# Row sums of a 67 MB array: loads of 14 rows per partition instead of 8, three buffers instead of five, and a re-cut end

## Chip, cores, metric

One core of a Trainium2 chip. The three groups of experiments below ran on three different chips (4, 11 and 0), each together with runs of the kernel before; so kernels of different groups are compared by their ratio to that kernel, or by their profiles. The metric is the device time of one execution in microseconds. Some executions of a kernel can fall into a slower state of the chip; every execution named here was in the fast state, except that the state of before_again, a single run, is unknown. The granted clock was 1.0 in all. The profile counts a shorter time, the span (162.9 us for an execution of 164.67 us before), so spans are compared with spans and times with times.

## The reference

```python
x: float32 [32, 512, 1024]          # 67.1 MB
out = np.sum(x, axis=-1) / 1024.0   # float32 [32, 512]
```

The 16,384 rows are laid out as 128 partitions of 128 consecutive rows. Each partition reads its own 512 KB of memory in order and writes 128 sums.

## The kernel before

The array is brought in by 21 loads: fifteen of 8 rows per partition, then 4, 2 and 1 rows, then the last row in three pieces. VectorE (DVE) sums 5 of each 8 rows with one reduction. ScalarE (ACT) sums the other 3 by a copy with an accumulator; the copies go to a scratch buffer in PSUM. SyncE (SP) issues all loads.

```python
bulk = [8] * 15
tail = [4, 2, 1]
pool = ctx.enter_context(tc.tile_pool(name="bulk", bufs=5))
psum = ctx.enter_context(tc.tile_pool(name="junk", bufs=1, space=bass.MemoryType.PSUM))
junk = psum.tile([P, D], F32, name="junk")
# ... cut ...
def act_sum(dst, src):
    n = src.shape[-1]
    nc.scalar.activation(junk[:, :n], src, COPY, accum_out=dst)

def sums(t, j, rows, for_act):
    d = rows - for_act
    if d:
        nc.vector.reduce_sum(out=res[:, j : j + d], in_=t[:, :d, :], axis=AX)
    for r in range(d, rows):
        act_sum(res[:, j + r : j + r + 1], t[:, r, :])

for rows in bulk:
    t = pool.tile([P, 8, D], F32, name="t")
    nc.sync.dma_start(out=t[:, :rows, :], in_=xr[:, j : j + rows, :])
    sums(t, j, rows, rows * 3 // 8)
    j += rows
# ... cut: the loads of 4, 2 and 1 rows, likewise ...
h, q = D // 2, D // 4
last = one.tile([P, D], F32, name="last")
for a, b in ((0, h), (h, h + q), (h + q, D)):
    nc.sync.dma_start(out=last[:, a:b], in_=xr[:, j, a:b])
nc.vector.reduce_sum(out=part[:, 0:1], in_=last[:, 0:h], axis=AX)
act_sum(part[:, 1:2], last[:, h : h + q])
nc.vector.tensor_scalar_mul(out=res[:, :j], in0=res[:, :j], scalar1=scale)
nc.vector.reduce_sum(out=part[:, 2:3], in_=last[:, h + q : D], axis=AX)
nc.vector.reduce_sum(out=part[:, 3:4], in_=part[:, 0:3], axis=AX)
nc.vector.tensor_scalar_mul(out=res[:, j : j + 1], in0=part[:, 3:4], scalar1=scale)
nc.sync.dma_start(out=out_v, in_=res)
```

Of the kernel before, what the change touches and what calls it, by code (L numbers as in the profile page):

```python
# [1 line left out]

# [4 lines left out]

F32 = mybir.dt.float32
ADD = mybir.AluOpType.add
MULT = mybir.AluOpType.mult  # L10
COPY = mybir.ActivationFunctionType.Copy
AX = mybir.AxisListType.X


@with_exitstack
def kernel(
    ctx: ExitStack,
    tc: tile.TileContext,
    x: bass.AP,
    divisor: float,  # L20
    out: bass.AP,
):
    nc = tc.nc
    xf = x.flatten_outer_dims()
    N, D = xf.shape
    P = nc.NUM_PARTITIONS
    scale = 1.0 / float(divisor)
    J = N // P
    assert J * P == N


    xr = x.tensor.reshape((P, J, D)).ap()
    out_v = out.tensor.reshape((P, J)).ap()

    bulk = [8] * 15
    tail = [4, 2, 1]
    assert sum(bulk) + sum(tail) + 1 == J
    pool = ctx.enter_context(tc.tile_pool(name="bulk", bufs=5))
    one = ctx.enter_context(tc.tile_pool(name="one", bufs=1))
    psum = ctx.enter_context(tc.tile_pool(name="junk", bufs=1, space=bass.MemoryType.PSUM))  # L40

    res = one.tile([P, J], F32, name="res")
    part = one.tile([P, 4], F32, name="part")
    junk = psum.tile([P, D], F32, name="junk")

    def act_sum(dst, src):
        n = src.shape[-1]
        nc.scalar.activation(junk[:, :n], src, COPY, accum_out=dst)  # L48

    def sums(t, j, rows, for_act):  # L50
        d = rows - for_act
        if d:
            nc.vector.reduce_sum(out=res[:, j : j + d], in_=t[:, :d, :], axis=AX)  # L53
        for r in range(d, rows):
            act_sum(res[:, j + r : j + r + 1], t[:, r, :])

    j = 0
    for rows in bulk:
        t = pool.tile([P, 8, D], F32, name="t")
        nc.sync.dma_start(out=t[:, :rows, :], in_=xr[:, j : j + rows, :])  # L60
        sums(t, j, rows, rows * 3 // 8)
        j += rows
    for k, rows in enumerate(tail):
        t = one.tile([P, rows, D], F32, name=f"tail{k}")
        nc.sync.dma_start(out=t, in_=xr[:, j : j + rows, :])
        sums(t, j, rows, (rows + 1) // 2)
        j += rows


    h, q = D // 2, D // 4  # L70
    last = one.tile([P, D], F32, name="last")
    for a, b in ((0, h), (h, h + q), (h + q, D)):
        nc.sync.dma_start(out=last[:, a:b], in_=xr[:, j, a:b])
    nc.vector.reduce_sum(out=part[:, 0:1], in_=last[:, 0:h], axis=AX)  # L74
    act_sum(part[:, 1:2], last[:, h : h + q])
    nc.vector.tensor_scalar_mul(out=res[:, :j], in0=res[:, :j], scalar1=scale)  # L76
    nc.vector.reduce_sum(out=part[:, 2:3], in_=last[:, h + q : D], axis=AX)  # L77
    nc.vector.reduce_sum(out=part[:, 3:4], in_=part[:, 0:3], axis=AX)  # L78
    nc.vector.tensor_scalar_mul(out=res[:, j : j + 1], in0=part[:, 3:4], scalar1=scale)  # L79
    nc.sync.dma_start(out=out_v, in_=res)  # L80


# [1 line left out]
_INS = ['x', 'divisor']  # L84
_OUTS = [((32, 512), 'float32')]

_NUMBERS = {'divisor': 1024.0}


# [26 lines left out]
```

## Time and profile before

| | before |
|---|---|
| time, median of 3 | 164.75 us (164.66 to 164.75) |
| span of the profiled execution | 162.9 us |
| load queue's share of the 16 DMA engines | 96.5% |
| DVE busy, ACT busy | 53%, 36% |
| one 8-row tile (4,096 KB) | each 9.71 us |
| last load landed (the trace's record of landings) / output issued | 159.31 / 160.41 us |

The first view is the profile's page for the kernel before: span, busy time, the DMA engines' busy tenths in 40 slices, the packets, the queue's share, the chain of waits by engine and line, and two groups of instructions. A group's columns are: line, engine, operation, output and input, shapes, count | busy time in us and mean ns of one | idle time before them in us, and what ended it.

```profile
span 162.9 us, 222 instructions
...
DVE 87.1 (53%) x22; ACT 58.1 (36%) x101; POOL 0.2 (0%) x4
...
DMA  6999999999999999999999999999999999999990
...
DMA packets 3169, 67.18 MB, mean 412 GB/s; under 512 B 352, under 2 KB 736, under 8 KB 992
...
q1 hardware_dynamic: 3168, 67.18, 96.5%
...
DMA 90%; DVE 7%; issue 1%; SPq 0%; DVEq 0%
DMA t<-in_x_dram 61%; DMA last<-in_x_dram 30%; DVE res L53 7%; DVE part L77 0%; DVE res L76 0%; DVE part L78 0%; DVE res L79 0%; SPq L60 0%; DVE part L74 0%; DVEq L78 0%
...
L53 DVE TENSOR_REDUCE res<-t 128x5 f32<-128x5120 f32 x15 | 82.3, 5488 | 72.5 <-DMA t<-in_x_dram 72.5
L48 ACT ACTIVATE junk<-t 128x1024 f32<-128x1024 f32 x45 | 46.2, 1027 | 99.2 <-DMA t<-in_x_dram 98.3
```

All but the first and the last slice have the DMA engines 90% busy or more. DVE waits 72.5 us and ACT 98.3 us for loads before these instructions. So neither of them bounds the kernel; the stream of loads does.

The second view is the timeline of the same kernel, in order of time: start in us, duration in us, engine, line, operation; in brackets, the idle time before and what ended it.

```profile
13.38 5.49 DVE L53 TENSOR_REDUCE res<-t 128x5 f32<-128x5120 f32 x1 [13.38 <-DMA t<-in_x_dram]
...
23.08 5.49 DVE L53 TENSOR_REDUCE res<-t 128x5 f32<-128x5120 f32 x1 [4.21 <-DMA t<-in_x_dram]
...
32.79 5.49 DVE L53 TENSOR_REDUCE res<-t 128x5 f32<-128x5120 f32 x1 [4.22 <-DMA t<-in_x_dram]
...
149.36 5.49 DVE L53 TENSOR_REDUCE res<-t 128x5 f32<-128x5120 f32 x1 [4.22 <-DMA t<-in_x_dram]
...
158.75 0.69 DVE L74 TENSOR_REDUCE part<-last 128x1 f32<-128x512 f32 x1 [0.59 <-DMA last<-in_x_dram]
...
159.36 0.22 DVE L76 TENSOR_SCALAR res<-res 128x127 f32<-128x127 f32 x1
159.49 0.41 DVE L77 TENSOR_REDUCE part<-last 128x1 f32<-128x256 f32 x1
...
160.00 0.15 DVE L78 TENSOR_REDUCE part<-part 128x1 f32<-128x3 f32 x1
160.19 0.15 DVE L79 TENSOR_SCALAR res<-part 128x1 f32<-128x1 f32 x1
160.41 0.35 SPq L80 DMA_DIRECT2D out_dram<-res  x1
```

The big reductions start 9.70 to 9.73 us apart, as each tile lands. Reducing takes 5.49 us of that. 4.19 MB in 9.71 us is 432 GB/s. The Trainium skill ("DMA: Bandwidth & Descriptors", section "Where 436 GB/s comes from") gives 435 GB/s as the ceiling of the fabric, and this trace agrees: there is under 1% between the two, and that 1% is what the change goes after. At the end, four small DVE instructions follow one another, and the output is issued at 160.41 us.

The trace also holds every DMA packet, with its size and its duration. In this kernel, each run of contiguous bytes of one partition is one packet: 1,920 of 32 KB for the fifteen bulk loads. The 128 packets of a load, shared by 16 DMA engines, are 8 for each. The medians, worked out from the trace (the last pieces' packets of 1 to 4 KB are left out):

| packet | count | median duration |
|---|---|---|
| 32 KB | 1,920 | 1,213 ns |
| 16 KB | 128 | 611 ns |
| 8 KB | 128 | 309 ns |
| 512 B (the output) | 128 | 27 ns |
| 4 B (completion of a load or of the output) | 352 | 9 ns |

### The profile page before, as it was taken

To read this page: it belongs to the slowest core of one execution; us is meant where nothing else is said; L and a number is where in the kernel's file an instruction comes from. 1 tells how busy PE (TensorE), PEld (TensorE's weight loads), DVE (VectorE), ACT (ScalarE), POOL (GpSimd) and SP (SyncE) were. 2 spreads that over 40 slices of the span, in tenths; PEclk is the share of its full clock that TensorE was granted. 3 is DMA by queue.
4 is the path that set the end of the run, shared out by engine and by line. 5 is a ranking of instruction groups with operands and counts; after the bars stand their busy time and mean duration, and the time that the engine had idled before them with its cause. 6 is when DMAs were issued, how large, how long until landed. Compare 5 with 4: busy or idle time off the path is not lost.

```text
span 162.9 us, 222 instructions
## 1 busy us (share of the span) xinstructions
DVE 87.1 (53%) x22; ACT 58.1 (36%) x101; POOL 0.2 (0%) x4
## 2 busy tenths in 40 slices
DVE  0007639094571917549093672908448092763983
ACT  3006135080531607034080622608043070613692
POOL 0000000000000000000000000000000000000000
DMA  6999999999999999999999999999999999999990
GB/s 209 426 418 443 435 435 435 418 443 435 410 459 426 402 467 435 394 459 435 426 443 418 435 437 418 443 435 410 443 443 402 459 443 410 443 435 398 408 352 16
DMA packets 3169, 67.18 MB, mean 412 GB/s; under 512 B 352, under 2 KB 736, under 8 KB 992
## 3 DMA queue, kind: packets, MB, share of 16 engines
q1 hardware_dynamic: 3168, 67.18, 96.5%
q14 instruction: 1, 0.01, 0.0%
HBM read 67.11 MB, written 0.07 MB: 412 GB/s over the span
## 4 chain that ended last, share of the span: by engine, by line
DMA 90%; DVE 7%; issue 1%; SPq 0%; DVEq 0%
DMA t<-in_x_dram 61%; DMA last<-in_x_dram 30%; DVE res L53 7%; DVE part L77 0%; DVE res L76 0%; DVE part L78 0%; DVE res L79 0%; SPq L60 0%; DVE part L74 0%; DVEq L78 0%
## 5 line engine op out<-in xcount | busy, mean ns | idle before, releaser
L53 DVE TENSOR_REDUCE res<-t 128x5 f32<-128x5120 f32 x15 | 82.3, 5488 | 72.5 <-DMA t<-in_x_dram 72.5
L48 ACT ACTIVATE junk<-t 128x1024 f32<-128x1024 f32 x45 | 46.2, 1027 | 99.2 <-DMA t<-in_x_dram 98.3
L48 ACT ACTIVATION_READ_ACCUMULATOR junk<-t 128x1 f32 x45 | 8.4, 186 | 0.0
L48 ACT ACTIVATE junk<-tail 128x1024 f32<-128x1024 f32 x4 | 4.1, 1028 | 1.7 <-DMA tail<-in_x_dram 1.7
L53 DVE TENSOR_REDUCE res<-tail 128x2 f32<-128x2048 f32 (+1 forms) x2 | 3.4, 1743 | 0.0
L48 ACT ACT_TABLE_LOAD x1 | 1.3, 1283 | 0.7 <-PEq L97 0.7
L74 DVE TENSOR_REDUCE part<-last 128x1 f32<-128x512 f32 x1 | 0.7, 685 | 0.6 <-DMA last<-in_x_dram 0.6
L48 ACT ACTIVATION_READ_ACCUMULATOR junk<-tail 128x1 f32 x4 | 0.7, 186 | 0.0
L77 DVE TENSOR_REDUCE part<-last 128x1 f32<-128x256 f32 x1 | 0.4, 411 | 0.0
L48 ACT ACTIVATE junk<-last 128x256 f32<-128x256 f32 x1 | 0.4, 388 | 0.0
L76 DVE TENSOR_SCALAR res<-res 128x127 f32<-128x127 f32 x1 | 0.2, 216 | 0.0
L78 DVE TENSOR_REDUCE part<-part 128x1 f32<-128x3 f32 x1 | 0.2, 155 | 0.1
L48 ACT ACTIVATION_READ_ACCUMULATOR junk<-last 128x1 f32 x1 | 0.2, 187 | 0.0
L79 DVE TENSOR_SCALAR res<-part 128x1 f32<-128x1 f32 x1 | 0.2, 154 | 0.0
L97 POOL MEMSET const-uint8-127<- 128x1 uint8 x1 | 0.1, 102 | 0.0
L97 POOL MEMSET const-bfloat16-1.0<- 128x1 bf16 x1 | 0.1, 101 | 0.0
L97 POOL MEMSET const-float32-0.0<- 128x1 f32 x1 | 0.1, 98 | 0.2 <-issue 0.2
L97 POOL MEMSET const-float32-1.0<- 128x1 f32 x1 | 0.1, 98 | 0.0
## 6 DMA issues: line engine op xcount, KB each, us to landing
t<-in_x_dram SPq DMA_DIRECT2D x15, 4096.0 KB, 43.0
tail<-in_x_dram SPq DMA_DIRECT2D x1, 2048.0 KB, 47.5
tail<-in_x_dram SPq DMA_DIRECT2D x1, 1024.0 KB, 49.5
tail<-in_x_dram SPq DMA_DIRECT2D x1, 512.0 KB, 50.4
last<-in_x_dram SPq DMA_DIRECT2D x1, 256.0 KB, 48.2
last<-in_x_dram SPq DMA_DIRECT2D x2, 128.0 KB, 34.1
out_dram<-res SPq DMA_DIRECT2D x1, 64.0 KB, 1.5
```

The source lines that it names most:

```text
L48: nc.scalar.activation(junk[:, :n], src, COPY, accum_out=dst)
L53: nc.vector.reduce_sum(out=res[:, j : j + d], in_=t[:, :d, :], axis=AX)
L74: nc.vector.reduce_sum(out=part[:, 0:1], in_=last[:, 0:h], axis=AX)
L76: nc.vector.tensor_scalar_mul(out=res[:, :j], in0=res[:, :j], scalar1=scale)
L77: nc.vector.reduce_sum(out=part[:, 2:3], in_=last[:, h + q : D], axis=AX)
L78: nc.vector.reduce_sum(out=part[:, 3:4], in_=part[:, 0:3], axis=AX)
L79: nc.vector.tensor_scalar_mul(out=res[:, j : j + 1], in0=part[:, 3:4], scalar1=scale)
L97: nc = _bacc.Bacc("TRN2", target_bir_lowering=False, num_devices=1)
```

## The change

Its intent: fewer and longer loads, so that less of the stream goes to fixed costs; a more even split of rows between the two engines; several scratch buffers for ACT; and fewer small pieces and fewer small instructions at the end. 21 loads become 14: eight of 14 rows (56 KB per partition), then 8, 4, 2 and 1 rows, then the last row in two pieces.

```diff
-    bulk = [8] * 15
-    tail = [4, 2, 1]
-    pool = ctx.enter_context(tc.tile_pool(name="bulk", bufs=5))
+    bulk = [14] * 7 + [14, 8]
+    split = {14: 6, 8: 4, 4: 2, 2: 1}      # rows that ACT takes
+    tail = [4, 2]
+    pool = ctx.enter_context(tc.tile_pool(name="bulk", bufs=3))
-    psum = ctx.enter_context(tc.tile_pool(name="junk", bufs=1, space=bass.MemoryType.PSUM))
+    psum = ctx.enter_context(tc.tile_pool(name="junk", bufs=4, space=bass.MemoryType.PSUM))
     def act_sum(dst, src):
+        junk = psum.tile([P, D], F32, name="junk")
         nc.scalar.activation(junk[:, :n], src, COPY, accum_out=dst)
# ... cut: sums() with the new split; loads kept in program order ...
-    for a, b in ((0, h), (h, h + q), (h + q, D)):
-        nc.sync.dma_start(out=last[:, a:b], in_=xr[:, j, a:b])
-    nc.vector.reduce_sum(out=part[:, 0:1], in_=last[:, 0:h], axis=AX)
-    act_sum(part[:, 1:2], last[:, h : h + q])
+    c = 704
+    t = one.tile([P, D], F32, name="row")
+    tc.keep_in_program_order(nc.sync.dma_start(out=t, in_=xr[:, j, :]))
+    act_sum(part[:, 0:1], t[:, c:])
+    nc.vector.reduce_sum(out=part[:, 1:2], in_=t[:, :c], axis=AX)
+    nc.vector.tensor_scalar(
+        out=res[:, j : j + 1], in0=part[:, 1:2], scalar1=part[:, 0:1], scalar2=scale, op0=ADD, op1=MULT
+    )
     nc.vector.tensor_scalar_mul(out=res[:, :j], in0=res[:, :j], scalar1=scale)
-    nc.vector.reduce_sum(out=part[:, 2:3], in_=last[:, h + q : D], axis=AX)
-    nc.vector.reduce_sum(out=part[:, 3:4], in_=part[:, 0:3], axis=AX)
-    nc.vector.tensor_scalar_mul(out=res[:, j : j + 1], in0=part[:, 3:4], scalar1=scale)
+    j += 1
+    t = one.tile([P, D], F32, name="last")
+    tc.keep_in_program_order(nc.sync.dma_start(out=t[:, :c], in_=xr[:, j, :c]))
+    tc.keep_in_program_order(nc.sync.dma_start(out=t[:, c:], in_=xr[:, j, c:]))
+    act_sum(part[:, 2:3], t[:, :c])
+    nc.vector.reduce_sum(out=part[:, 3:4], in_=t[:, c:], axis=AX)
+    nc.vector.tensor_scalar(
+        out=res[:, j : j + 1], in0=part[:, 3:4], scalar1=part[:, 2:3], scalar2=scale, op0=ADD, op1=MULT
+    )
```

More of the change, by code (lines that the diff above doesn't have):

```diff
@@ L33 @@
     out_v = out.tensor.reshape((P, J)).ap()
-    bulk = [8] * 15
-    tail = [4, 2, 1]
-    assert sum(bulk) + sum(tail) + 1 == J
-    pool = ctx.enter_context(tc.tile_pool(name="bulk", bufs=5))
+    bulk = [14] * 7 + [14, 8]
+    split = {14: 6, 8: 4, 4: 2, 2: 1}
+    tail = [4, 2]
+    assert sum(bulk) + sum(tail) + 2 == J
+    pool = ctx.enter_context(tc.tile_pool(name="bulk", bufs=3))
     one = ctx.enter_context(tc.tile_pool(name="one", bufs=1))
-    psum = ctx.enter_context(tc.tile_pool(name="junk", bufs=1, space=bass.MemoryType.PSUM))
+    psum = ctx.enter_context(tc.tile_pool(name="junk", bufs=4, space=bass.MemoryType.PSUM))
@@ L42, with sums @@
     res = one.tile([P, J], F32, name="res")
     part = one.tile([P, 4], F32, name="part")
-    junk = psum.tile([P, D], F32, name="junk")
     def act_sum(dst, src):
         n = src.shape[-1]
+        junk = psum.tile([P, D], F32, name="junk")
         nc.scalar.activation(junk[:, :n], src, COPY, accum_out=dst)
-    def sums(t, j, rows, for_act):
-        d = rows - for_act
-        if d:
-            nc.vector.reduce_sum(out=res[:, j : j + d], in_=t[:, :d, :], axis=AX)
+    def sums(t, j, rows):
+        d = rows - split[rows]
@@ L54, in sums @@
         for r in range(d, rows):
             act_sum(res[:, j + r : j + r + 1], t[:, r, :])
+        nc.vector.reduce_sum(out=res[:, j : j + d], in_=t[:, :d, :], axis=AX)
     j = 0
-    for rows in bulk:
-        t = pool.tile([P, 8, D], F32, name="t")
-        nc.sync.dma_start(out=t[:, :rows, :], in_=xr[:, j : j + rows, :])
-        sums(t, j, rows, rows * 3 // 8)
+    for i, rows in enumerate(bulk):
+        t = pool.tile([P, 14, D], F32, name="t")
+        tc.keep_in_program_order(nc.sync.dma_start(out=t[:, :rows, :], in_=xr[:, j : j + rows, :]))
+        sums(t, j, rows)
@@ L62 @@
         j += rows
-    for k, rows in enumerate(tail):
-        t = one.tile([P, rows, D], F32, name=f"tail{k}")
-        nc.sync.dma_start(out=t, in_=xr[:, j : j + rows, :])
-        sums(t, j, rows, (rows + 1) // 2)
+    for i, rows in enumerate(tail):
+        t = one.tile([P, rows, D], F32, name=f"tail{i}")
+        tc.keep_in_program_order(nc.sync.dma_start(out=t, in_=xr[:, j : j + rows, :]))
+        sums(t, j, rows)
         j += rows
-    h, q = D // 2, D // 4
-    last = one.tile([P, D], F32, name="last")
@@ L80 @@
-    nc.sync.dma_start(out=out_v, in_=res)
+    c = 704
[6 more added lines that the diff above has]
+    )
+    nc.vector.tensor_scalar_mul(out=res[:, :j], in0=res[:, :j], scalar1=scale)
+    j += 1
@@ new lines @@
+    t = one.tile([P, D], F32, name="last")
[6 more added lines that the diff above has]
+    )
+    tc.keep_in_program_order(nc.sync.dma_start(out=out_v, in_=res))
```

## The prediction

> **What bounds it now.** The loads. The page gives the load queue 96.5% of the 16 DMA engines' span, DVE 53%, ACT 36%; the chain of waits is 90% DMA. In order of time, a 4,096 KB tile lands every 9.71 us (reductions start at 13.38, 23.08, 32.79 ... 149.36 us), so 4.19 MB / 9.71 us = 432 GB/s. The Trainium skill (DMA: Bandwidth & Descriptors, "Where 436 GB/s comes from") puts the fabric's ceiling at 435 GB/s; this trace agrees. DVE needs 5.49 us and ACT 3.5 us of each 9.71; both wait for loads (groups: idle 72.5 and 98.3 us). SyncE's buffer waits (99 us) starve nothing: transfers land 43 us after issue, so over 30 us stay queued.
>
> **Sum for the span of 162.9 us.** First packet 1.74; stream until the last load lands at about 159.3; last reductions and final scale until the output's issue at 160.41; its landing and the end, 2.5. The measured time adds 1.9 (164.75).
>
> **What the change does.**
> 1. Fewer, longer transfers: 21 loads become 14, runs per partition grow from 32 KB to 56 KB. The trace's packets by size: 32 KB takes 1,213 ns, 16 KB 611, 8 KB 309, 512 B 27: about 9 ns fixed per packet plus bytes at 27.2 GB/s. Each load has 8 packets per DMA engine and a 4-byte completion of 9 ns: about 0.083 us per load (estimate from these). Seven fewer save 0.58 us of stream, all on the critical path, if 56 KB stays one packet (then some 2.12 us). If it is cut in two, the saving is nearly nil.
> 2. Three 56 KB buffers (168 KB per partition) for five of 32 KB (160 KB). A 14-row tile should land each 16.95 us; DVE takes 8 rows in about 8.7 us (1.04 ns per element plus 0.15 us, fitted to 5,488 and 685 ns), ACT 6 rows in 7.1 us (1.18 each). The buffer is handed back about 9 us after landing with two tiles, some 34 less 9 us of transfers, still queued. No bubble. The first tile lands at about 20.6 rather than 13.4 us, at no cost.
> 3. The new split and four PSUM scratch buffers: off the critical path.
> 4. The end. After the 8-row tile, landings should come 4.9, 2.5, 1.3, 0.9 and 0.45 us apart. DVE (4.4, 2.3, 1.2, then scale 0.2 + 704 elements 0.89 + combine 0.15) and ACT (4.7, 2.4, 1.2, 0.6) each keep up. After the last 320 columns land: reduce 0.49, gap 0.08, combine 0.15, so the output's issue follows by about 0.8 us; ACT's 704 columns (0.76 + 0.19) end at about the same time. Before, it is about 1.1 us. Saves 0.3.
>
> **Predicted: 163.9 us**, 0.5% faster; range 163.4 to 164.5. Faster by over 2%: 0.01; within 2%: 0.98; slower by over 2%: 0.01.
>
> **What would show it.** Page: span near 162.0; 2,160 packets on the load queue, 1,024 of them 56 KB; load queue still 96 to 97%. Chain: DMA still about 90%. Timeline: big reductions 16.95 us apart, about 8.7 us long; last load at about 158.7; output issued at about 159.6.
>
> **What would make it wrong.** 56 KB runs cut into several packets or read more slowly (then 164.4 or above); a slower first transfer; a load issued late; the engines not keeping up over the last 5 us, since the 8-row tile's ACT share (4.7 us) nearly fills its 4.9 us gap.

## The result

| | before | changed |
|---|---|---|
| time, median of 4 | 164.75 us (164.66 to 165.13) | 164.17 us (163.95 to 164.42) |
| single times | 164.75, 164.75, 164.66, 165.13 | 164.42, 164.38, 163.95, 163.96 |
| span of the profiled execution | 162.89 us | 162.65 us |
| stream, first packet to last load landed | 157.57 us | 157.61 us |
| last load landed to output issued | 1.10 us | 0.88 us |

The ratio is 0.9961, with a 95% interval of 0.9936 to 0.9985: faster by 0.4%, and within 2% as predicted. Here and below, a ratio is the ratio of the fast runs of a kernel to those of the kernel before in the same rounds; it is close to the ratio of the means, but not quite that, nor that of the medians quoted.

The time lies inside the predicted range. But the profile does not show what was predicted: in this execution (164.42 us, the slowest of the four) the stream is no shorter than before, and nearly the whole difference in span (0.24 us) is that of the end (0.22 us). So the right total could have had the wrong reasons, and that is what the experiments are about.

The page of the changed kernel, the lines that answer to those above:

```profile
span 162.6 us, 213 instructions
...
DVE 79.3 (49%) x16; ACT 61.1 (38%) x115; POOL 0.2 (0%) x4
...
DMA packets 2161, 67.18 MB, mean 413 GB/s; under 512 B 240, under 2 KB 496, under 8 KB 752
...
q1 hardware_dynamic: 2160, 67.18, 96.5%
...
DMA 74%; DVE 18%; another core or an unknown queue 5%; SPq 1%; issue 0%; DVEq 0%
DMA t<-in_x_dram 48%; DMA tail<-in_x_dram 25%; DVE res L56 17%; DVE part L75 0%; SPq L61 0%; SPq L66 0%; DVE part L87 0%; DVE res L79 0%; DVE res L88 0%; DVE res L76 0%; DVEq L88 0%; DVEq L76 0%; DVEq L79 0%
...
L56 DVE TENSOR_REDUCE res<-t 128x8 f32<-128x8192 f32 (+1 forms) x9 | 73.9, 8212 | 79.9 <-DMA t<-in_x_dram 79.9
L50 ACT ACTIVATE junk<-t 128x1024 f32<-128x1024 f32 x52 | 52.5, 1009 | 96.7 <-DMA t<-in_x_dram 96.7
```

The packets on the load queue are the predicted 2,160, and the share of the DMA engines is the predicted 96 to 97%. The chain of waits is not as predicted: 18% of it is DVE. Whether that DVE time matters is tested below. The timeline of the same execution:

```profile
20.63 8.69 DVE L56 TENSOR_REDUCE res<-t 128x8 f32<-128x8192 f32 x1 [20.63 <-DMA t<-in_x_dram]
...
37.80 8.69 DVE L56 TENSOR_REDUCE res<-t 128x8 f32<-128x8192 f32 x1 [8.49 <-DMA t<-in_x_dram]
...
54.87 8.69 DVE L56 TENSOR_REDUCE res<-t 128x8 f32<-128x8192 f32 x1 [8.38 <-DMA t<-in_x_dram]
...
71.97 8.69 DVE L56 TENSOR_REDUCE res<-t 128x8 f32<-128x8192 f32 x1 [8.41 <-DMA t<-in_x_dram]
...
88.87 8.69 DVE L56 TENSOR_REDUCE res<-t 128x8 f32<-128x8192 f32 x1 [8.22 <-DMA t<-in_x_dram]
...
156.81 1.22 DVE L56 TENSOR_REDUCE res<-tail 128x1 f32<-128x1024 f32 x1 [0.21 <-DMA tail<-in_x_dram]
...
158.14 0.23 DVE L79 TENSOR_SCALAR res<-res 128x126 f32<-128x126 f32 x1
...
158.28 0.88 DVE L75 TENSOR_REDUCE part<-row 128x1 f32<-128x704 f32 x1
...
159.27 0.21 DVE L76 TENSOR_SCALAR res<-part 128x1 f32<-128x1 f32 x1
159.40 0.47 DVE L87 TENSOR_REDUCE part<-last 128x1 f32<-128x320 f32 x1
...
159.98 0.21 DVE L88 TENSOR_SCALAR res<-part 128x1 f32<-128x1 f32 x1
160.22 0.35 SPq L91 DMA_DIRECT2D out_dram<-res  x1
```

Tiles two, three and four come 17.17, 17.07 and 17.10 us after the one before them; then they come 16.90 to 16.96 us apart. 16.95 was predicted. The early three are late by about 0.5 us in total. In the trace's packets of this execution, the median 56 KB packet takes 2,116 ns, as predicted, but 120 packets after the first 4 us are over 40 ns slower than 9 ns plus their bytes at 27.2 GB/s, 112 of them between 23 and 70 us. Their excess comes to 0.60 us for each engine (the sum over all packets, divided by 16). I call these "slow packets" below, always with this definition.

### The profile page after: what moved, and what is told of

It is laid out like the page before. It is cut to its first block, busy times and chain, and to the rows that moved or that the text cites. A ratio compares the mean times of both kernels' runs of the same rounds, so it can differ in the third digit from the quotient of the medians.

```text
span 162.6 us, 213 instructions
## 1 busy us (share of the span) xinstructions
DVE 79.3 (49%) x16; ACT 61.1 (38%) x115; POOL 0.2 (0%) x4
## 3 DMA queue, kind: packets, MB, share of 16 engines
q1 hardware_dynamic: 2160, 67.18, 96.5%
## 4 chain that ended last, share of the span: by engine, by line
DMA 74%; DVE 18%; another core or an unknown queue 5%; SPq 1%; issue 0%; DVEq 0%
DMA t<-in_x_dram 48%; DMA tail<-in_x_dram 25%; DVE res L56 17%; DVE part L75 0%; SPq L61 0%; SPq L66 0%; DVE part L87 0%; DVE res L79 0%; DVE res L88 0%; DVE res L76 0%; DVEq L88 0%; DVEq L76 0%; DVEq L79 0%
## 5 line engine op out<-in xcount | busy, mean ns | idle before, releaser
L56 DVE TENSOR_REDUCE res<-t 128x8 f32<-128x8192 f32 (+1 forms) x9 | 73.9, 8212 | 79.9 <-DMA t<-in_x_dram 79.9
L50 ACT ACTIVATE junk<-t 128x1024 f32<-128x1024 f32 x52 | 52.5, 1009 | 96.7 <-DMA t<-in_x_dram 96.7
L50 ACT ACTIVATION_READ_ACCUMULATOR junk<-t 128x1 f32 x52 | 9.7, 186 | 0.0
L50 ACT ACTIVATE junk<-tail 128x1024 f32<-128x1024 f32 x3 | 3.1, 1022 | 0.9 <-DMA tail<-in_x_dram 0.9
L50 ACT ACTIVATE junk<-last 128x704 f32<-128x704 f32 x1 | 0.8, 761 | 0.3 <-DMA last<-in_x_dram 0.3
L75 DVE TENSOR_REDUCE part<-row 128x1 f32<-128x704 f32 x1 | 0.9, 880 | 0.0
L87 DVE TENSOR_REDUCE part<-last 128x1 f32<-128x320 f32 x1 | 0.5, 475 | 0.0
L79 DVE TENSOR_SCALAR res<-res 128x126 f32<-128x126 f32 x1 | 0.2, 228 | 0.1
L88 DVE TENSOR_SCALAR res<-part 128x1 f32<-128x1 f32 x1 | 0.2, 214 | 0.1
L76 DVE TENSOR_SCALAR res<-part 128x1 f32<-128x1 f32 x1 | 0.2, 214 | 0.1
```

The costliest lines, as they stand in the source:

```text
L75: nc.vector.reduce_sum(out=part[:, 1:2], in_=t[:, :c], axis=AX)
L76: nc.vector.tensor_scalar(out=res[:, j : j + 1], in0=part[:, 1:2], scalar1=part[:, 0:1], scalar2=scale, op0=ADD, op1=MULT)
L87: nc.vector.reduce_sum(out=part[:, 3:4], in_=t[:, c:], axis=AX)
L88: nc.vector.tensor_scalar(out=res[:, j : j + 1], in0=part[:, 3:4], scalar1=part[:, 2:3], scalar2=scale, op0=ADD, op1=MULT)
```

## The experiments

My theory (theory 1) was this: fewer packets do save about 0.5 us of stream, the end saves 0.2 us, and slow packets, which come and go between executions, hid the first saving in the profiled run. The main rival (theory 2) was that long packets save nothing and that the end is the whole gain. A second rival was that the gain comes from the faster ACT or from the buffers. Eleven runs were made, in three groups (the first four, the next four and the last three rows below the first two); each group shares its runs of the kernel before.

| run | time, median (range) | ratio to before | stream | slow packets, us per engine | landed to output issued |
|---|---|---|---|---|---|
| before, first profile | 164.75 (164.66 to 165.13) | | 157.57 | 0.18 | 1.10 |
| changed, first profile | 164.17 (163.95 to 164.42) | 0.9961 | 157.61 | 0.60 | 0.88 |
| after_again | 163.94 (163.85 to 164.17) | 0.9952 | 157.05 | 0.05 | 0.87 |
| end_only | 164.61 (164.47 to 164.75) | 0.9987 | 157.69 | 0.02 | 0.89 |
| bulk_only | 164.30 (164.24 to 164.62) | 0.9975 | 157.70 | 0.57 | 1.04 |
| row_packets | 170.19 (170.13 to 170.33) | 1.0327 | 163.28 | 0.02 | 0.86 |
| half_packets | 164.66 (164.56 to 164.88) | 0.9991 | 157.71 | 0.25 | 0.86 |
| seven_loads | 164.55 (164.37 to 164.59) | 0.9981 | 157.79 | 0.02 | 0.86 |
| one_scratch | 164.28 (163.80 to 164.51) | 0.9964 | 157.49 | 0.37 | 0.90 |
| two_buffers | 164.24 (163.86 to 164.41) | 0.9961 | 157.06 | 0.09 | 0.88 |
| before_again | 164.77 (one run) | | 157.74 | 0.13 | 1.03 |
| row_576 | 164.03 (163.96 to 164.21) | 0.9957 | 157.25 | 0.29 | 0.86 |
| tile_contiguous (wrong result) | 163.79 (163.62 to 164.07) | 0.9943 | 156.97 | 0.05 | 0.86 |

The first two columns of numbers are of all the fast runs, in us and as a ratio; the last three are in us and belong to the one profiled execution of each kernel. The kernel before had medians of 164.74, 164.78 and 164.74 us in the three groups, with single runs from 164.62 to 165.20.

### after_again: the changed kernel, unedited

> The changed kernel, unedited, to see its spread. In its profiled run the loads took 157.61 us from first packet to last landing, against 157.58 before, so none of the 0.58 us that fewer packets should save showed; between 23 and 70 us some hundred of the 56 KB packets took 40 to 240 ns longer than their usual 2,116. Theory 1: fewer packets save 0.58 us of stream, and slow packets, which differ from run to run, ate most of it in that run; then times spread from 163.9 (clean) to 164.5, and a profile shows that first tiles come 16.95 us apart when no packets are slow, and late by exactly the sum of the slow ones otherwise. Theory 2: 56 KB packets gain nothing and the whole gain is that of the end of the program; then the stream is 157.6 us in every profile, and the times stay at 164.2 to 164.5.

Measured: 163.94 us, five runs from 163.85 to 164.17. This execution had few slow packets (0.05 us per engine). The timeline of this run:

```profile
20.58 8.69 DVE L56 TENSOR_REDUCE res<-t 128x8 f32<-128x8192 f32 x1 [20.58 <-DMA t<-in_x_dram]
...
37.49 8.69 DVE L56 TENSOR_REDUCE res<-t 128x8 f32<-128x8192 f32 x1 [8.22 <-DMA t<-in_x_dram]
...
54.43 8.69 DVE L56 TENSOR_REDUCE res<-t 128x8 f32<-128x8192 f32 x1 [8.26 <-DMA t<-in_x_dram]
```

The tiles come 16.91 to 16.95 us apart, and the stream is 157.05 us, 0.56 us less than in the first profile of the same kernel; the slow packets differ by 0.60 less 0.05, 0.55 us. So the slow packets match in size what the first profile had lost, and theory 2's constant 157.6 us is refuted. A spread of this size shows in single runs of both kernels. The match is not this close everywhere. From the first reduction to the ninth, this profile takes 128.26 us; the first profile, one_scratch, row_576 and two_buffers take 0.53, 0.45, 0.14 and 0.21 us more, with 0.55, 0.32, 0.24 and 0.04 us more of slow packets. So the sum of the slow packets tells the lost time to some 0.2 us; it is a mean over 16 engines, and a tile waits for all of its 16 completions.

### end_only and bulk_only: each half of the change alone

```diff
# end_only, against the changed kernel
-    bulk = [14] * 7 + [14, 8]
+    bulk = [8] * 15
-    pool = ctx.enter_context(tc.tile_pool(name="bulk", bufs=3))
+    pool = ctx.enter_context(tc.tile_pool(name="bulk", bufs=5))
-        t = pool.tile([P, 14, D], F32, name="t")
+        t = pool.tile([P, 8, D], F32, name="t")
# bulk_only, against the kernel before
-    bulk = [8] * 15
+    bulk = [14] * 8 + [8]
-    pool = ctx.enter_context(tc.tile_pool(name="bulk", bufs=5))
+    pool = ctx.enter_context(tc.tile_pool(name="bulk", bufs=3))
-        t = pool.tile([P, 8, D], F32, name="t")
+        t = pool.tile([P, 14, D], F32, name="t")
```

> The new end (4, 2, 1 rows and two last pieces, 4 and 4 rows of the 8-row tiles for each engine, four scratch buffers) with the old bulk of fifteen 8-row loads in five buffers. 20 loads for 21. Theory 1 (packets and end each give a part): stream shorter by 0.08 us, output issued about 0.87 us after the last landing rather than 1.09; about 164.45 us, span 162.6. Theory 2 (all the gain is the end): about 164.2 us, the same as the whole change.

> The 14-row loads in three buffers alone; the old end (4, 2, 1 rows, three last pieces) and one scratch buffer. 15 loads for 21. Theory 1: stream shorter by 0.5 us where no packets are slow, so 164.25 us, and up to 164.7 where they are; 56 KB packets of 2,116 ns. Theory 2: 164.7 us, as before.

Measured: the end alone gives 164.61 us against 164.74 of the same rounds, and the longer loads alone 164.30 us. Theory 2 asked for about 164.2 and 164.7: it has the two the wrong way round. Theory 1 asked for 164.45 and for 164.25 to 164.7. Of the five runs of bulk_only, three took 164.24 to 164.30 us and two 164.61 and 164.62; its profiled execution is one of these two, with 0.57 us of slow packets. So both parts give something, and by the medians the loads give more. The ratios' intervals (0.9961 to 0.9988 for the loads, 0.9975 to 1.0 for the end) overlap, so these times alone do not settle which part is larger; but each excludes what theory 2 asked of it, no gain from the loads and the whole gain from the end.

The sizes do not add up exactly: 0.44 and 0.13 us make 0.57, while the whole change gave 0.80 us in the same rounds. In end_only's profile the output was issued 0.89 us after the last landing, as in the whole change, but its stream was 157.69 us with hardly a slow packet, about 0.4 us more than 157.57 less 0.18 (slow packets of before) less 0.08 us (for one load fewer) lets expect. The timelines say where it went. The first tile was reduced 0.13 us later (13.51 us against 13.38). From the first to the fifteenth big reduction both profiles take the same, 135.97 and 135.98 us, although before had 0.16 us more of slow packets: those had cost its tiles nothing that shows, and should not have been subtracted. And the time from the last big reduction's start to the last landing is 9.93 against 9.95 us, so the one load fewer saved hardly anything that shows. Why the first tile comes at a slightly different time in each execution stays open; single executions of a kernel differ by 0.3 to 0.6 us here.

### row_packets: many more packets, the same loads

```diff
-        t = pool.tile([P, 14, D], F32, name="t")
-        ... dma_start(out=t[:, :rows, :], in_=xr[:, j : j + rows, :])
-        sums(t, j, rows)
+        t = pool.tile([P, 14, D + 16], F32, name="t")
+        ... dma_start(out=t[:, :rows, :D], in_=xr[:, j : j + rows, :])
+        sums(t[:, :, :D], j, rows)
```

The unused elements break up the contiguous run in the buffer, so that each row becomes a packet.

> The changed kernel with 16 unused elements after each row of the bulk buffers, so that each bulk load is cut into packets of one row, 4 KB (888 more packets for each of the 16 engines, as many loads and as many bytes, the work of the engines the same). If the stream pays about 9.5 ns for each packet (theory 1), it gets 8.4 us longer and the time is about 172.6 us, with 4 KB packets of some 160 ns. If the packets' fixed time is hidden, or is a cost of each load rather than of each packet, the time stays at 164.2 us (rival).

Measured: 170.19 us, 6.25 us more than the changed kernel in the same rounds. First the page's count of packets for this run, then a part of its timeline:

```profile
DMA packets 16369, 67.18 MB, mean 399 GB/s; under 512 B 240, under 2 KB 496, under 8 KB 16112
```

```profile
21.34 8.69 DVE L56 TENSOR_REDUCE res<-t 128x8 f32<-128x8192 f32 x1 [21.34 <-DMA t<-in_x_dram]
...
39.03 8.69 DVE L56 TENSOR_REDUCE res<-t 128x8 f32<-128x8192 f32 x1 [9.01 <-DMA t<-in_x_dram]
```

Packets do cost time, with loads, bytes and the engines' work unchanged; the rival (no change) is out. The tiles come 17.69 us apart (median), 0.75 us more than 16.94, over 104 more packets for each engine: 7.2 ns for each. That is less than the expected 9.5 ns. The reason is in the trace: the packets' durations, summed over the loads, make 165.5 us for each engine, but the stream from first packet to last landing is only 163.3 us. So, in this run, consecutive packets of one engine must overlap a little, and the duration of a packet is not quite what it costs the stream.

### half_packets and seven_loads: a cost of packets or of loads?

```diff
# half_packets, against the changed kernel: one load, two runs per partition
-        t = pool.tile([P, 14, D], F32, name="t")
+        t = pool.tile([P, 2, 7 * D + 16], F32, name="t")
+        h = rows // 2
-        ... dma_start(out=t[:, :rows, :], in_=xr[:, j : j + rows, :])
+        ... dma_start(out=t[:, :, : h * D], in_=xr[:, j : j + rows, :] as [P, 2, h * D])
# ... cut: ACT sums the second half, DVE the first (7 and 7 rows instead of 6 and 8) ...
# seven_loads, against the changed kernel: two loads, the buffer as it was
-        ... dma_start(out=t[:, :rows, :], in_=xr[:, j : j + rows, :])
+        for a in range(0, rows, rows // 2):
+            b = a + rows // 2
+            ... dma_start(out=t[:, a:b, :], in_=xr[:, j + a : j + b, :])
```

> The changed kernel with 16 unused elements in the middle of each bulk buffer, so that each bulk load goes out as two packets per partition (28 KB, or 16 KB for the 8-row tile) instead of one: 72 more packets for each DMA engine, as many loads and bytes. The 4 KB packets of the earlier run cost 7.1 ns each by the tiles' spacing (17.68 less 16.94 us over 104 packets), less than the 9.5 ns of the prediction. Theory 1, cost by packet: 72 times 7.1 ns is 0.51 us, so 164.4 to 164.5 us against 163.94. Rival, a cost of each load or of long packets as such: 163.9 us still.

> The changed kernel with each bulk tile brought by two loads of half its rows, into the same buffer: the packets of the run with halved packets (28 and 16 KB, 72 more for each engine), and 9 more loads with their completions. If nearly all of the cost is by packet, as theory 1 has it (57 of the 75 ns that a load costs, by the spacing of 8-row and 14-row tiles), then 0.51 + 9 x 0.018 = 0.67 us above 163.94, about 164.6 us. If it is by load (rival: 0.075 us each and packets free), 164.6 us as well, but then the run with halved packets is at 163.9.

Measured: 164.66 us (half_packets) and 164.55 us (seven_loads). The count of packets and two lines of each timeline, half_packets first:

```profile
DMA packets 3313, 67.18 MB, mean 413 GB/s; under 512 B 240, under 2 KB 496, under 8 KB 752
...
122.77 7.62 DVE L69 TENSOR_REDUCE res<-t 128x7 f32<-128x7168 f32 x1 [9.39 <-DMA t<-in_x_dram]
...
139.80 7.62 DVE L69 TENSOR_REDUCE res<-t 128x7 f32<-128x7168 f32 x1 [9.41 <-DMA t<-in_x_dram]
```

```profile
DMA packets 3457, 67.18 MB, mean 413 GB/s; under 512 B 384, under 2 KB 640, under 8 KB 896
...
20.69 8.69 DVE L56 TENSOR_REDUCE res<-t 128x8 f32<-128x8192 f32 x1 [20.69 <-DMA t<-in_x_dram]
...
37.71 8.69 DVE L56 TENSOR_REDUCE res<-t 128x8 f32<-128x8192 f32 x1 [8.33 <-DMA t<-in_x_dram]
```

With 72 more packets and as many loads, the kernel gives nearly the whole gain back. Adding 9 loads to those packets adds nothing that shows. So the cost is the packet's, and the rival (a cost of each load) is out. Another rival, that the unused elements in the buffer cost the time and not the number of packets, is out for these sizes too: seven_loads has no unused elements and the same spacing. The size: tiles come 17.03 and 17.02 us apart (medians), 0.09 and 0.08 us more than 16.94, for 8 more packets per engine and tile. That is 10 to 11 ns for each, and the ratios (0.9991 and 0.9981 against 0.9952) make 0.64 and 0.48 us over 72 packets, 9 and 7 ns. Against two_buffers, which ran on the same chip (0.9961), the ratios make 0.49 and 0.33 us, 7 and 5 ns. So a packet costs 5 to 11 ns; the spacing, 10 to 11 ns, is the closest reading. My expectation for half_packets, 164.4 to 164.5 us, used 7.1 ns and was too low; the 9 ns of the prediction would have served better.

### one_scratch and two_buffers: the parts called off the critical path

```diff
# one_scratch, against the changed kernel
-    psum = ctx.enter_context(tc.tile_pool(name="junk", bufs=4, space=bass.MemoryType.PSUM))
+    psum = ctx.enter_context(tc.tile_pool(name="junk", bufs=1, space=bass.MemoryType.PSUM))
# two_buffers, against the changed kernel
-    pool = ctx.enter_context(tc.tile_pool(name="bulk", bufs=3))
+    pool = ctx.enter_context(tc.tile_pool(name="bulk", bufs=2))
```

> The changed kernel with one scratch buffer in PSUM instead of four. ACT's rows should then start 1.18 us apart, as before the change, instead of 1.04. If that and the split of rows lie off the critical path, as predicted, the time stays at 163.9 to 164.1 us; if the changed kernel's gain came partly from a faster ACT (rival), it loses 0.1 us or more, most of it in the last 5 us, where ACT's 4 rows take 4.7 us of the 4.9 us until the next tile lands.

> The changed kernel with two bulk buffers instead of three. By point 2 of the prediction a buffer comes free 9 us after its tile landed, while the next tile's 16.94 us of transfers are still on the engines, so some 8 us of work stays queued and the time stays at 163.9 to 164.1 us. If the depth of the queue matters (rival), the transfers stall once a tile: any gap between tiles of over 16.95 us shows it, and nine gaps of only 0.1 us would make it 164.8 us.

Measured: 164.28 and 164.24 us, with fastest runs of 163.80 and 163.86 us; the changed kernel had 163.85. The ratios, 0.9964 and 0.9961, are at the upper of the two that the changed kernel itself gave (0.9961 and 0.9952), well within the intervals. The medians are 0.1 to 0.2 us above what I expected and 0.3 us above after_again's, in another group of rounds, so the times alone don't exclude the rivals. The profiles say more. First ACT's rows in the timeline of one_scratch, then in that of the changed kernel:

```profile
20.60 1.03 ACT L50 ACTIVATE junk<-t 128x1024 f32<-128x1024 f32 x1 [18.59 <-DMA t<-in_x_dram]
...
21.78 1.03 ACT L50 ACTIVATE junk<-t 128x1024 f32<-128x1024 f32 x1
```

```profile
20.63 1.03 ACT L50 ACTIVATE junk<-t 128x1024 f32<-128x1024 f32 x1 [18.62 <-DMA t<-in_x_dram]
...
21.68 1.01 ACT L50 ACTIVATE junk<-t 128x1024 f32<-128x1024 f32 x1
```

With one scratch buffer, ACT starts a row 1.18 us after the one before, all through; with four, 1.05 us after the first and then each 1.04 us. Yet one_scratch issues its output 0.90 us after the last landing, against 0.87 and 0.88, and its late stream (157.49 us) goes with 0.37 us of slow packets. In two_buffers the stream is 157.06 us and the tiles are 16.93 to 16.95 us apart but for one gap of 17.10, so handing a buffer back with one tile queued instead of two costs nothing that shows. The one gap is over the 16.95 us that were to betray a stall, but the trace shows no stall in it: at every moment of it at least 15 packets were in flight, for 16 engines, and one of its packets was 0.37 us late. A third buffer is spare here.

### row_576: is the end bound by DVE or by the last landing?

```diff
-    act_sum(part[:, 0:1], t[:, c:])                                    # row before the last; c = 704
-    nc.vector.reduce_sum(out=part[:, 1:2], in_=t[:, :c], axis=AX)
+    act_sum(part[:, 0:1], t[:, 576:])
+    nc.vector.reduce_sum(out=part[:, 1:2], in_=t[:, :576], axis=AX)
```

> The changed kernel with 128 columns of the last row but one moved from VectorE to ScalarE (split at 576 instead of 704). The chain of waits shows VectorE without a gap from 156.81 us on, as if it bounded the end; but the last piece lands at about the moment VectorE is free. If the landing bounds (theory 1), the output is still issued 0.86 to 0.88 us after the last landing; if VectorE does (rival), it is issued 0.13 us earlier, 0.74 us after it. The time can show no more than 0.1 us: 163.8 to 164.3.

Measured: 164.03 us, and the output is issued 0.86 us after the last landing, as theory 1 has it. The chain of waits of this run, by line:

```profile
DMA t<-in_x_dram 48%; DMA last<-in_x_dram 26%; DVE res L56 16%; SPq L66 1%; ACT junk L50 0%; SPq L61 0%; SPq L73 0%; DVE res L88 0%; ACTq L122 0%; ACTq L50 0%
```

It goes from the last combine (L88) to ACT's share of the last row and from there to the load of that row. In the changed kernel it went through L79, L75 and L76 of DVE to the 2-row load instead, which looked as if DVE were the limit. The timeline of row_576 shows why that was no limit:

```profile
158.65 0.76 ACT L50 ACTIVATE junk<-last 128x704 f32<-128x704 f32 x1 [0.22 <-DMA last<-in_x_dram]
...
158.99 0.49 DVE L87 TENSOR_REDUCE part<-last 128x1 f32<-128x320 f32 x1
...
159.59 0.21 DVE L88 TENSOR_SCALAR res<-part 128x1 f32<-128x1 f32 x1
```

ACT waits 0.22 us for its piece of the last row. DVE is done with the row before at 158.96 us (158.75 and 0.21), and its own piece lands at 158.97. Both engines then finish within 0.06 us of each other (159.48 and, with the accumulator's read, 159.54 us). So the landings bound the end on both sides. In the changed kernel DVE's path and the landing tie, and a chain has to pick one; taking 0.13 us off the one it had picked won nothing.

### before_again and tile_contiguous: where do slow packets come from?

```diff
# tile_contiguous, against the changed kernel; the sums come out in the wrong places, on purpose
-        ... dma_start(out=t[:, :rows, :], in_=xr[:, j : j + rows, :])
+        ... dma_start(out=t[:, :rows, :], in_=xf[j * P : (j + rows) * P].rearrange("(p r) d -> p r d", r=rows))
```

> The kernel before, unedited, for a second profile. If slow packets come and go between executions of any kernel, as theory 1 has it, this one differs from the first (42 packets over 40 ns late after the first 4 us, 0.18 us for each engine): its last load lands at 159.31 us less 0.18 plus whatever this execution has of them, and its 8-row tiles come 9.71 us apart. The output is issued 1.10 us after the last landing, as in the first profile.

> Wrong result on purpose: the bulk tiles of the changed kernel take 7 MB of consecutive memory each, so that neighbouring partitions read 56 KB apart instead of 512 KB; packets, loads, bytes and the engines' work as in the changed kernel; the sums land in the wrong places of the output. Question: what makes the slow packets, which came in some executions of the changed kernel (0.05 to 0.60 us for each engine). If the 512 KB step between partitions makes engines collide in memory, they vanish: six executions within 0.1 us of 163.85, and no packets over 40 ns late after the first 4 us. If they come from outside the kernel, the times spread as before, from 163.8 to 164.5.

Measured: before_again had 32 slow packets, 0.13 us per engine, so the kernel before has them too. Its last load landed at 159.47 us, where the expectation makes 159.26: late by 0.2 us that slow packets do not explain. Its output was issued 1.03 us after the landing. tile_contiguous took 163.62 to 164.07 us: four of its five listed runs lie within 0.2 us, but not within the 0.1 us asked for, and one is 0.3 us later. Its profile has 0.05 us of slow packets, no fewer than after_again. So a step of 512 KB between partitions is not shown to make them, nor cleared. It costs nothing steady: the tiles come 16.94 us apart (median) either way. The cause of slow packets stays open.

## Why the prediction was right, point by point

- **What bounds the kernel.** Right. The stream of loads bounds it before and after: slowing ACT, taking away a buffer and moving work between the engines changed nothing clear, and adding packets did at once.
- **Fewer packets save 0.58 us of stream.** Right in mechanism and a little large. The spacing of tiles gives 9.71 us for 8 rows and 16.94 for 14, so a row is 1.205 us and a load's fixed part, nearly all of it that of its 8 packets, is 0.07 us (predicted: 0.083). Seven loads fewer make 0.5 us. As a check: the two clean streams of the long loads (after_again and two_buffers, 157.05 and 157.06 us) are 0.60 us shorter than the two of before (157.57 and 157.74); less the difference in slow packets (0.15 against 0.07 us on average) that leaves 0.5 us (0.6 if, as end_only suggests, the slow packets of before cost it nothing); under 0.1 us of it is due to the last pieces, one fewer than before. The 56 KB runs did stay one packet of 2,116 ns (predicted: 2.12 us), and half_packets showed the fallback of the prediction: cut in two, nearly all the saving is gone.
- **Three buffers make no bubble.** Right. DVE took 8.69 us for 8 rows (predicted: 8.7), and even two buffers made no bubble that shows. ACT took 1.04 us for a row and not 1.18, so 6 rows took 6.2 us, not 7.1: I kept the old pace and missed what four scratch buffers do. It was off the critical path, so the miss cost nothing.
- **The end saves 0.3 us.** Mis-sized. From last landing to output it took 1.10 and 1.03 us in the two profiles of before, and 0.87 to 0.88 in the two of the changed kernel: 0.15 to 0.23 us. The term that failed is the "combine 0.15": I took the 154 ns of the old final scale, but the new instruction has a second operation, an add with a per-partition operand, and takes 214 ns. Whether the operation or the operand makes it longer was not tested. The wait before it was 0.11 us, where I had 0.08.
- **The predicted time, 163.9 us.** The median was 164.17 at first and 163.94 in the second set. The terms measured are 0.5 us for the stream and 0.2 for the end, against 0.58 and 0.3; slow packets add 0 to 0.5 us to the executions profiled. The range alone would have shown little: theory 2's 164.2 to 164.5 us lies in it as well, so it took the experiments to show that the terms were right. What the prediction left out is that spread: the profiled execution met 0.60 us of slow packets, and so "span near 162.0" (162.65) and "tiles 16.95 us apart" (17.17 at first) failed there and held in the second profile (162.07; 16.91 to 16.95).
- **The chain of waits, "DMA still about 90%".** Wrong: 74%, and 18% DVE. The chain runs through three of the 8.69 us reductions, two of which released the buffer of a later load, and at the end through DVE instead of the load that arrived at the same moment. Neither cost time, as two_buffers and row_576 show. The 5% of "another core or an unknown queue" is a stretch of 8.35 us that the profile could put down to nothing.

## What to carry to other kernels

This stream of loads already ran within 1% of the 435 GB/s cited above, and what was left to gain in it was the fixed part of each packet. The layout of the buffer and the cut into loads decided the number of packets, so where a kernel looks like this one it is worth keeping what one partition receives contiguous, and long (here up to 56 KB, which stayed one packet). Read the cost of a packet from the spacing of landings when their number is changed, not from the packet's own duration (7.2 against 9.5 ns in row_packets). And when an effect is 0.5%, one profile is not enough: the first one here showed a stream no shorter than before, although the saving was real, because that execution met slow packets.

## What the Trainium skill lacked or had wrong

- "HBM Reference", section "Specifications (TRN2)", has about 425 GB/s for a core streaming alone, bounded by its DMA engines; "DMA: Bandwidth & Descriptors", section "Where 436 GB/s comes from", says that for transfers between HBM and SBUF the HBM side (about 358) binds. Here one core read from HBM at 432 GB/s (4.19 MB each 9.71 us), and at 433 GB/s with 56 KB packets (7.34 MB each 16.94 us). The 358 did not bind; the first page gives it for both cores of a pair streaming, which no run here does, so it is the second page's sentence, without that condition, that these runs contradict. As a mean over the whole stream (67.1 MB in 157.57 us before, 426 GB/s) the 425 holds; the 432 is the steady pace.
- "DMA: Bandwidth & Descriptors", section "Rules for kernel authors", asks for 1 MiB or more per load. It sets no length for the packets inside such a load, and what the page says of a fixed cost for each packet is about small ones: at 7 MB per load, cutting the runs from 56 KB to 4 KB cost 6.25 us of 164 (7.0 ns for each of 888 more packets per engine), and cutting them in two cost 0.5 to 0.65 us (by the ratios of seven_loads and half_packets).
- No page that I looked up has the slower pace of accumulating copies on ACT that all write one PSUM buffer: 1.18 us a row of 1,024 with one buffer, against 1.04 with four.
- No page that I looked up has the time of a short DVE scale-and-add on 128 x 1 elements: 214 ns with a per-partition operand, where the scale alone with a constant took 154.
- No page that I looked up has the executions in which many packets run more than 40 ns late for tens of microseconds (0.02 to 0.60 us per engine and execution).
